# Attention values in transposed float32r form, with the order of all instructions from the kernel's own list schedule

## The chip, the cores and the metric

The kernel runs on one core of a Trainium2 chip. The metric is the device time of one execution in microseconds. Three runs of the kernel before took 700.12, 702.43 and 703.76 us; their median is 702.43 us.

## The reference

One layer of a hybrid decoder, float32, 512 tokens of 1024 features. Cut to what matters here:

```python
h = modulate(rms_norm(x, pre_norm_mix), sh1, sc1)          # shift and scale from silu(c) @ ada_w + ada_b
z = h @ w_in                                               # gate, x, q, 3 x (k, v), attention gates
rnn = gelu(g_rnn) * rg_lru(conv4(x_rnn))
# attention: 8 query heads, 2 key/value heads of 64 features; three branches, each with its own softmax
o = g0 * softmax(q kc^T - alibi) @ vc                      # 31 compressed blocks of keys
  + g1 * softmax(q ks^T - alibi) @ vs                      # selected blocks: all 8 of the 8, causal
  + g2 * softmax(q kw^T - alibi) @ vw                      # window of 512: all, causal
y = concat([rms_norm(rnn, norm_rnn_out), rms_norm(att, norm_att_out)]) @ w_out
x = x + (1 + g1) * rms_norm(y, post_norm_mix)
h = modulate(rms_norm(x, pre_norm_mlp), sh2, sc2)
x = x + (1 + g2) * rms_norm(square(relu(h @ w_ff1)) @ w_ff2, post_norm_mlp)
```

With 512 tokens the top 16 blocks of 64 are all 8 blocks, so the selected branch is plain causal attention.

## The kernel before

All large products are made in parts: a float32 operand is split into a high and a low part in float32r (`split_f32`, line 399), and `mm3` (line 762) sums high x high, high x low and low x high in PSUM. The eight PSUM banks have four names: `f` (2), `s` (3), `pv` (1), `tp` (2).

The work has five stages: a first wave (`first_wave`, line 689: norm of x, modulation, and the first columns of the input projection, bound to the arrival of the modulation's weights); then projections, recurrent branch, attention and output projection; then the MLP's first product (`up_first`, `up`), its second (`down_all`), and the last norm (`finish`).

Attention is cut into 16 units, in the order of `UNITS`: a key head g, a tile i of 128 tokens, and a pair of query heads. `att_scores` (line 1194) makes for each head of the pair the scores of the three branches side by side (compressed, selected, window), with the mask and the slope added and the row maxima taken by VectorE (`mx`), then `Exp` on ScalarE with the row sums in `sm`. `den` is the gate over the row sum. The probabilities `p` lie with tokens on partitions and are not normalised. `att_values` (line 1249) transposes blocks of 128x128 of `p` on TensorE into a bank `tp`, up to four blocks a bank, and `evac` (line 472) copies them to `pt` in float32 on ScalarE or VectorE, whichever is sooner free. The product takes `pt` as the stationary operand and moves a block of values, 64 columns, float32; it leaves tokens on partitions, and the three branches and two heads side by side in one bank `pv`. VectorE multiplies the bank by `den` into `tmp`, and GpSimd adds the three branches into `att`. At most two units are scored ahead of the values. `att_finish` (line 1297) takes the sum of squares of a tile of `att` by `Square` with accumulation, transposes the tile, and ScalarE and VectorE write the high and low parts with the norm's gain (`Q[k]`, `Q[4 + k]`, whose buffers are free by then). `projections` (line 924) multiplies these by `w_out`; the residual and the second norm follow, and `turn_h` (line 1331) transposes the result and writes the MLP's input in parts `h2` and `h2l`.

The order: class `Clocks` (line 51) keeps an estimated time for each engine. Every instruction goes through `issue` (line 167), by `mm` (216), `turn` (222), `act` (225), `elem` (236) or `load` (266), each with a cost formula. `pace` (line 203) doubles TensorE's cost in a window that follows an idle one. Streams (generators) of instructions are chosen by `run_streams` (line 291) for the one TensorE can start first; `Weights` (line 316) runs loads and splits ahead of use. After the first wave instructions are recorded, and `flush` (line 118) emits them by a key: 0.7 of the estimated start less 0.3 of the length of the longest chain that follows. There are three flushes: after the attention, after the first MLP columns, and at the end. Up to the end of the first wave the kernel holds the tile framework's manual schedule open (`start_ctx`), so that this part stays in the order of emission; after it the framework's scheduler orders what it is given. Each engine then runs its own queue in that order.

Of the kernel before, what the change touches and what calls it, by code (L numbers as in the profile page):

```python
# [38 lines left out]
# the order of the input projection's columns and of the compression's weights, and that of the attention's units  # L39
# [4 lines left out]
# sets of activation tables that have a function  # L44
# [3 lines left out]
WINDOW = 4096 / 1200.0  # L48


class Clocks:
    """What each engine has been given so far, in estimated microseconds: every instruction goes through here
    on its way to the engine, and the order of emission is chosen by these clocks."""

    def __init__(self, nc):
        self.nc = nc
        self.free = dict.fromkeys(("pe", "act", "dve", "pool", "dma", "dge"), 0.0)
        self.boxes = {}
        self.base = {}
        self.slots = {}  # L60
        self.table = None
        self.windows = {}
        self.nodes = None
        self.name = ""
        self.uses = {}
        self.before = {}

    # -- tiles --
    def tile(self, pool, tag, bufs, shape, dtype, name):
# [3 lines left out]
        if len(ring) < bufs:  # L73
            self.base[key] = 0.0
        else:
            old = ring.pop(0)
            self.base[key] = self.last(old)
            self.boxes.pop(old, None)
            self.before[key] = old
# [25 lines left out]
    def ready(self, *aps):  # L105
        """when what these hold has been written"""
# [11 lines left out]
    def flush(self):  # L118
        """emit what was recorded, what has most left to come first"""
        nodes, self.nodes = self.nodes, []  # L120
        tail = [0.0] * len(nodes)
        for k in range(len(nodes) - 1, -1, -1):
            eng, cost, prev = nodes[k][:3]
            tail[k] += cost
            for j in prev:
                lag = (SYNC if nodes[j][0] != eng else 0.0) + (DMA_LAT if nodes[j][0] == "dma" else 0.0)
                tail[j] = max(tail[j], tail[k] + lag)
        left = [0] * len(nodes)
        after = [[] for _ in nodes]
        for k, (_, _, prev, _, _, _) in enumerate(nodes):  # L130
            left[k] = len(prev)
            for j in prev:
                after[j].append(k)
        key = [(1 - TAIL) * start - TAIL * tail[k]
               for k, (_, _, _, _, start, _) in enumerate(nodes)]
        heap = [(key[k], k) for k in range(len(nodes)) if not left[k]]
        heapq.heapify(heap)
        while heap:
            _, k = heapq.heappop(heap)
            nodes[k][3]()  # L140
            for j in after[k]:
                left[j] -= 1
                if not left[j]:
                    heapq.heappush(heap, (key[j], j))
        self.uses, self.before = {}, {}

    def put(self, eng, cost, outs, ins, fn):
# [3 lines left out]
        for ap, wr in [(a, False) for a in ins] + [(a, True) for a in outs]:  # L151
            key = ap.tensor.name
            if key not in self.uses:
                self.uses[key] = []
                for u in self.uses.get(self.before.get(key), ()):
                    prev.add(u[5])
# [8 lines left out]
        self.nodes.append((eng, cost, prev, fn, self.start, self.name))  # L165

    def issue(self, eng, cost, outs, ins, fn):
        start = self.free[eng]
        for ap, wr in [(a, False) for a in ins] + [(a, True) for a in outs]:
# [13 lines left out]
        if eng == "pe":  # L183
            cost = self.pace(start, cost)
        end = start + cost
        self.start = start
# [16 lines left out]
    def pace(self, start, cost):  # L203
        """the tensor engine's clock is halved in a window that follows an idle one"""
        k = int(start / WINDOW)
        if self.windows.get(k - 1, 0.0) < 0.5 * WINDOW:
            cost *= 2
        end = start + cost
        while start < end:
            stop = min(end, (k + 1) * WINDOW)  # L210
            self.windows[k] = self.windows.get(k, 0.0) + stop - start
            start, k = stop, k + 1
        return cost

    # -- instructions --
    def mm(self, out, lhs, rhs, start, stop):
        n = out.free_size()
        fast = 1 if rhs.dtype == F32R and n >= 256 else 4
        self.issue("pe", max(n * fast / 2400 + 0.002, 0.1 if fast == 4 else 0.05), [out], [lhs, rhs],
                   lambda: self.nc.tensor.matmul(out, lhs, rhs, start=start, stop=stop))  # L220

    def turn(self, out, src, ident):
        self.issue("pe", out.free_size() / 1175, [out], [src], lambda: self.nc.tensor.transpose(out, src, ident))  # L223

    def act(self, out, src, func, scale=1.0, bias=0.0, accum_out=None):
        ins = [src] + [a for a in (scale, bias) if not isinstance(a, float)]
        outs = [out] + ([accum_out] if accum_out is not None else [])
        cost = 0.05 + out.free_size() / 1200 + 0.043 * (src.space != PSUM) + 0.05 * (len(ins) + len(outs) - 2)
        if func in TABLES and self.table not in TABLES[func]:
# [4 lines left out]
                   lambda: self.nc.scalar.activation(out, src, func, scale=scale, bias=bias, **kw))  # L234

    def elem(self, eng, what, out, *args, **kw):
# [11 lines left out]
        else:  # L248
            cost = 0.165 + n / (480 if len(wide) > 1 else 1000)
# [16 lines left out]
    def load(self, out, src):  # L266
        self.free["dge"] = max(self.free["dge"], 0.0) + 0.47
        self.free["dma"] = max(self.free["dma"], self.free["dge"])
        self.issue("dma", out.free_size() * out.shape[0] * 4 / 360000.0, [out], [src],
# [3 lines left out]
class Stream:  # L273
    """A generator of instructions. Before each step it yields a function for when that step can start."""
# [41 lines left out]
class Weights:  # L316
    """The weights in the order of their use: loads ahead of splits into high and low parts, both ahead of use."""

    def __init__(self, clk, pool):
        self.clk, self.pool, self.jobs, self.index = clk, pool, [], {}  # L320
# [4 lines left out]
    def add(self, name, n, loads, split=True):  # L325
        self.index[name] = len(self.jobs)
        self.jobs.append((name, n, loads, split))
# [21 lines left out]
    def load(self):  # L349
# [4 lines left out]
        self.loaded[name] = raw  # L354
        self.raw_live.append(name)
        self.l += 1

    def split(self):
# [3 lines left out]
        if split:  # L362
            hi = c.tile(self.pool, "hi", PART_BUFS, [P, 1024], F32R, f"hi_{name}")[:, :n]
            lo = c.tile(self.pool, "lo", PART_BUFS, [P, 1024], F32R, f"lo_{name}")[:, :n]
            split_f32(c, hi, lo, raw[:, :n])
            self.parts[name] = (hi, lo)
            self.raw_live.remove(name)
            self.part_live.append(name)
# [13 lines left out]
    def when(self, name, k=None):  # L382
        """when the weights of a job can be used"""
# [10 lines left out]
    def drop(self, name):  # L394
        """nothing more reads this job's tiles"""
        (self.part_live if self.jobs[self.index[name]][3] else self.raw_live).remove(name)


def split_f32(c, hi, lo, src):
    """src = hi + lo exactly, both with the short mantissa of float32r"""  # L400
# [12 lines left out]
def block_kernel(tc, x, c, ada_w, ada_b, pre_norm_mix, w_in, conv_w, conv_b, lru_wa, lru_ba, lru_wx,  # L413
# [52 lines left out]
    def p_tile():  # L466
        return small(mp, "p", 4, [P, K_END])

    def pt_tile(dt):
        return small(mp, "pt", 4, [P, 512], dt)  # L470
# [13 lines left out]
    def after(ev, fn=None):  # L484
        """a step's start: once an event has happened, and then what fn says"""
# [28 lines left out]
    # k - q, with the mask of the future; the same for the compressed keys  # L514
# [10 lines left out]
    # tokens that see a whole compressed block  # L525
# [23 lines left out]
    def rstd_of(ss, width):  # L549
        """(ss / width + eps) ** -0.5"""  # L550
# [8 lines left out]
    V = [mp.tile([P, 4, 64], F32, name=f"V{t}") for t in range(NT)]  # L559
    VC = [mp.tile([32, 64], F32, name=f"VC{g}") for g in range(2)]  # L560
# [32 lines left out]
    for hf_ in range(2):  # L593
        for n in range(2):
            for k2 in range(2):
                r0 = hf_ * 512 + k2 * 256
                W.add(f"o{hf_}{n}{k2}", 1024, [(lambda r: r.rearrange("p (k c) -> p k c", k=2),
                                               w_out[r0:r0 + 256, half(n)].rearrange("(k p) c -> p k c", p=P))])
# [6 lines left out]
    def norm_x(t, h=None):  # L605
        """the squares' sum of a tile of tokens (half h of it), then the tile normed, features 0 first"""
# [19 lines left out]
    def warm(n):  # L626
        """keep the tensor engine's clock up while the first norm waits for its data"""
# [26 lines left out]
    def ada_sums(j):  # L654
        """shift and scale of features j, from the sums of the rows of each partition"""
# [16 lines left out]
    def prep_h(j, at, pt, sa, rest=None):  # L672
        """the tokens' features j, modulated; the sums for the next ones in between"""
# [85 lines left out]
    start_ctx.close()  # L759
# [35 lines left out]
    # rows (parity of the token, feature), columns (k or v, group, token)  # L795
# [54 lines left out]
    def values():  # L850
        for t in range(NT):
# [13 lines left out]
            act(V[t], src, AF.Copy)  # L865
# [5 lines left out]
    def compress(v, l4):  # L871
        """hidden units of the compressed keys and values, transposed"""
# [15 lines left out]
    def compress_out():  # L888
# [12 lines left out]
        for g in range(2):  # L901
            act(VC[g], pc2[:32, 64 * g:64 * g + 64], AF.Copy)
# [21 lines left out]
    def projections():  # L924
        for hf_ in range(2):
# [561 lines left out]
```

## Time and profile before

| | |
|---|---|
| runs | 700.12, 702.43, 703.76 us |
| span of the profiled execution (the only time that it has) | 700.8 us |
| instructions in the profile | 9072 |
| DMA | 85.10 MB, 121 GB/s mean |
| attention's value products | 384 instructions of 64 columns, two for each of 192 products |
| transposes of probabilities | 192 |

Engines are PE (TensorE), PEld (its weight loads), DVE (VectorE), ACT (ScalarE), POOL (GpSimd) and SP (SyncE, which issues the transfers). A row of a group is: line, engine, operation, names out<-in, shapes, count | busy us, mean ns | idle time of the engine just before, with what ended it. The names are those of the tiles, without numbers. Most instructions have the line of a helper (L220 matmul, L223 transpose, L234 ScalarE, L255 VectorE and GpSimd), so the tile names tell them apart. A row of a window is: from:to and its length, busy us and count for PE, PEld, DVE, ACT and POOL, the granted clock of TensorE (1.00 is full speed), the DMA share, GB/s. A row of the timeline is: start, duration, engine, line, operation, names, count, and in brackets the idle time before it. A row of the chain is: start, us, engine, tile and line, count. Banks `f`, `s`, `pv` and `tp` appear in products of several stages.

### The profile page before, as it was taken

Reading aid. Unit: us, or ns where it says so; the run is one execution under the profiler, and the core shown is the slowest. Engines: PE = TensorE matmul, PEld = TensorE weight load, DVE = VectorE, ACT = ScalarE, POOL = GpSimd, SP = SyncE. Lnnn points to the kernel's source line nnn. Section 1 sums busy time; section 2 is a strip of 40 time slices with the busy share of each in tenths; the row PEclk is TensorE's granted clock in tenths of the full one; section 3 lists DMA queues with packets and bytes.
Section 4 is the critical chain, followed back from the end, with each engine's and each line's share of the span. In section 5 each row is a group of like instructions: output and inputs, shape, how many; then the busy total and the mean of one; then the engine's idle time right before and its main releaser. Section 6 shows DMA issues by size and latency. Waiting matters only on the chain.

```text
span 700.8 us, 9072 instructions
## 1 busy us (share of the span) xinstructions
PE 654.4 (93%) x3350; PEld 543.0 (77%) x3350; DVE 414.2 (59%) x788; ACT 267.6 (38%) x553; POOL 157.9 (23%) x148
## 2 busy tenths in 40 slices
PE   3888899894999999998899999999999999999995
PEld 3666788474888889897898888888888888888884
DVE  5998974678688856684895374343353333333334
ACT  4335424584686665565441111111122332222221
POOL 4232010337225201222234343333410000000001
PEclk9999999897999999999999999999999999999999
DMA  8985668642435510001556353432323222223102
GB/s 272 271 249 158 181 206 235 206 130 85 132 111 157 201 35 27 1 0 55 157 151 180 90 151 93 118 91 91 102 97 101 91 91 90 91 91 96 55 18 102
DMA packets 89971, 85.10 MB, mean 121 GB/s; under 512 B 5172, under 2 KB 71876, under 8 KB 89928
## 3 DMA queue, kind: packets, MB, share of 16 engines
q1 hardware_dynamic: 89928, 84.54, 39.6%
q8 instruction: 26, 0.43, 0.3%
q14 instruction: 17, 0.14, 0.1%
HBM read 82.43 MB, written 2.10 MB: 121 GB/s over the span
## 4 chain that ended last, share of the span: by engine, by line
PE 49%; DVE 1%; ACT 0%; issue 0%; POOL 0%; DVEq 0%; POOLq 0%
PE f L220 28%; PE s L220 11%; PE tp L220 7%; PE pv L220 4%; DVE r L255 1%; PE tp L223 0%; ACT ar L234 0%; POOL stat L255 0%; ACT r L234 0%; DVEq L1483 0%; POOLq L1483 0%; DVE h2l L255 0%; DVE stat L255 0%
## 5 line engine op out<-in xcount | busy, mean ns | idle before, releaser
L220 PE MATMUL f<-h,hi_f 128*128 128x512 f32 x224 | 83.4, 393 | 0.0
L220 PE MATMUL f<-h,lo_f 128*128 128x512 f32 x224 | 82.7, 389 | 0.0
L220 PE MATMUL f<-h2l,hi_f 128*128 128x512 f32 x224 | 82.6, 389 | 0.0
L255 POOL TENSOR_TENSOR fT<-fT 128x512 f32<-128x512 f32 x32 | 57.9, 1812 | 107.3 <-ACT fT L234 107.3
L255 DVE TENSOR_TENSOR fl<-fT,fh 128x512 fp32r<-128x512 f32 x28 | 19.3, 690 | 88.1 <-ACT fh L234 88.1
L234 ACT ACTIVATE fT<-f 128x512 f32<-128x512 f32 x28 | 16.8, 600 | 126.1 <-PE f L220 126.1
L234 ACT ACTIVATE fh<-fT 128x512 fp32r<-128x512 f32 x28 | 17.7, 632 | 105.1 <-PE f L220 103.3
L255 POOL TENSOR_SCALAR stat<-stat 128x1 f32<-128x1 f32 (+1 forms) x21 | 7.8, 373 | 218.7 <-DVE stat L255 182.3
L255 DVE CAST hi_f<-raw_f 128x1024 fp32r<-128x1024 f32 x24 | 18.0, 749 | 63.5 <-PE f L220 63.5
L234 ACT ACTIVATE p<-p,mx 128x32 f32<-128x32 f32 (+4 forms) x96 | 45.3, 473 | 26.1 <-DVE mx L255 25.9
L255 DVE SCALAR_TENSOR_TENSOR accT<-ar,sil,accT 128x512 f32<-128x512 f32 x56 | 50.0, 892 | 6.5 <-DMA ar<-in_ada_w 5.9
L255 DVE TENSOR_TENSOR lo_d<-raw_d,hi_d 128x1024 fp32r<-128x1024 f32 x32 | 40.2, 1255 | 15.7 <-ACT hi_d L234 15.3
L220 PEld LDWEIGHTS f<-h,hi_f 128*128 128x128 f32 x224 | 42.1, 188 | 9.1 <-issue 0.5
L220 PEld LDWEIGHTS f<-h2l,hi_f 128*128 128x128 f32 x224 | 42.0, 188 | 9.1 <-issue 0.5
L220 PEld LDWEIGHTS f<-h,lo_f 128*128 128x128 f32 x224 | 42.1, 188 | 8.8
L220 PEld LDWEIGHTS pv<-V,pt 128*128 128x128 f32 x320 | 44.8, 191 | 2.9 <-ACT pt L234 0.5
L220 PE MATMUL pv<-V,pt 128*128 128x64 f32 x320 | 44.4, 260 | 0.2 <-ACT pt L234 0.2
L220 PE MATMUL s<-K,Q 128*128 128x288 f32 (+4 forms) x128 | 35.3, 346 | 9.5 <-DVE mx L255 9.5
L255 DVE TENSOR_TENSOR lo_f<-raw_f,hi_f 128x1024 fp32r<-128x1024 f32 x30 | 40.7, 1357 | 3.9 <-ACT hi_f L234 1.3
L223 PE MATMUL tp<-ident,p 128*128 128x128 f32 (+1 forms) x192 | 40.6, 279 | 0.7 <-DVE h L255 0.7
L220 PE MATMUL s<-hi_d,fh 128*128 128x512 f32 x84 | 33.3, 396 | 0.0
L220 PE MATMUL s<-hi_d,fl 128*128 128x512 f32 x84 | 33.3, 396 | 0.0
(259 smaller groups left out, 1607.4 us busy)
## 6 DMA issues: line engine op xcount, KB each, us to landing
ar<-in_ada_w SPq DMA_DIRECT2D x32, 512.0 KB, 5.4
raw_f<-in_w_ff SPq DMA_DIRECT2D x32, 512.0 KB, 4.1
raw_d<-in_w_ff SPq DMA_DIRECT2D x32, 512.0 KB, 3.2
p<-in_ada_w SPq DMA_DIRECT2D x32, 256.0 KB, 3.8
raw_o<-in_w_out SPq DMA_DIRECT2D x8, 512.0 KB, 4.3
r<-in_x SPq DMA_DIRECT2D x7, 512.0 KB
raw_a<-in_w_in SPq DMA_DIRECT2D x8, 320.0 KB, 5.2
raw_x<-in_w_in SPq DMA_DIRECT2D x4, 512.0 KB
```

The source lines that it names most:

```text
L220: lambda: self.nc.tensor.matmul(out, lhs, rhs, start=start, stop=stop))
L223: self.issue("pe", out.free_size() / 1175, [out], [src], lambda: self.nc.tensor.transpose(out, src, ident))
L234: lambda: self.nc.scalar.activation(out, src, func, scale=scale, bias=bias, **kw))
L255: self.issue(eng, cost, outs, ins, lambda: fn(out, *args, **kw))
```

## The change

1. **Scaling first.** After `den`, each of the three branches of both heads' `p` is multiplied by its column of `den` (`scaled`), on GpSimd, VectorE or ScalarE, by the clocks. That is 96 instructions: 49 on VectorE, 29 on ScalarE, 18 on GpSimd.
2. **Values transposed.** V and the compressed values VC are kept as high and low parts side by side, 128 columns in float32r. Per block the two heads' probabilities are transposed beside each other (at most two blocks, 512 columns, in a bank); ScalarE writes the high part, VectorE the bank less the high part. The product takes the values (64 columns high, 64 low) as the stationary operand and moves the high, then the low part of the probabilities, 256 columns for two heads; all three branches add up in one accumulation. Partitions 0 to 63 hold what the high part of the values gave, partitions 64 to 127 what the low part gave: ScalarE copies the latter out (`oc`), and VectorE adds both into `att`, which now has features on partitions.
3. **The end of the attention.** `att` needs no transpose any more. ScalarE squares it, GpSimd adds, and a product with a column of ones gives the sum of squares. The gain of the norm goes into the split of the weights of the output projection (`gains` in `Weights`).
4. **Buffers.** Six tiles of `p` and `pt` instead of four, four of `mx`, `sm` and `den` instead of three; up to three units ahead.
5. **Order.** `flush` is a list schedule: it runs all engines by estimated time, each takes from what is ready the instruction with the longest chain after it, and ScalarE avoids a change of its function table. `pace` is gone, the cost formulas have other constants. The manual schedule stays open to the end, so the order of emission is the order of the queues. The first wave keeps its order. After it TensorE goes through pairs of projection columns in alternation; in the MLP's first product the two banks `f` advance in alternation and end close together (before, most of one came first); in the second each column's 24 products go through all eight banks three times, high x high, then low x high, then high x low; at the end the two halves of the last tokens finish together.

```diff
     def flush(self):
...
+        for _ in range(n - first):
+            best = None
+            for e, t in self.real.items():
+                if soon[e]:
+                    at = t
+                elif wait[e]:
+                    at = max(t, wait[e][0][0])
+                else:
+                    continue
+                if best is None or at < best[0]:
+                    best = at, e
+            at, e = best
+            while wait[e] and wait[e][0][0] <= at + 0.01:
+                _, k = heapq.heappop(wait[e])
+                heapq.heappush(soon[e], (-tail[k], k))
+            if e == "act":
+                k = self.pick_act(soon[e], nodes)
+            else:
+                _, k = heapq.heappop(soon[e])
...
+            self.real[e] = self.fin[k] = at + cost
             nodes[k][3]()
...
+    def scaled(seg, col):
+
+        n, f = seg.free_size(), clk.free
+        r = clk.ready(seg, col)
+        cost = {"pool": 0.165 + n / 1000, "dve": 0.125 + n / 1900, "act": 0.14 + n / 1200}
+        eng = min(cost, key=lambda e: max(f[e], r) + cost[e])
+        if eng == "act":
+            act(seg, seg, AF.Copy, scale=col)
+        else:
+            clk.elem(eng, "tensor_scalar", seg, seg, col, None, op0=ALU.mult)
...
     def att_values():
...
-                    for k, (e, _, c0, _, _, _) in enumerate(sub):
-                        turn(tp[:w, tok(k)], scored[u][0][e][:, c0:c0 + w], ident)
-                    pt = pt_tile(F32)[:w, :P * len(sub)]
-                    evac(pt, tp[:w, :P * len(sub)])
-                    turned.append((pt, sub))
+                    for k, (c0, _) in enumerate(sub):
+                        for e in range(2):
+                            turn(tp[:, tok(2 * k + e)], scored[u][e][:, c0:c0 + P], ident)
+                    w = 256 * len(sub)
+                    hi, lo = pt_tile(F32R)[:, :w], pt_tile(F32R)[:, :w]
+                    act(hi, tp[:, :w], AF.Copy)
+                    dve("tensor_sub", lo, tp[:, :w], hi.bitcast(F32))
+                    turned.append((hi, lo, sub))
...
-                    for k, (e, si, _, v, first, last) in enumerate(sub):
-                        mm(po[:, si, e, :], pt[:, tok(k)], v, first, last)
-            den = scored[u][1]
-            tmp = small(mp, "tmp", 2, [P, 3, 2, 64])
-            dve("tensor_mul", tmp, po, den.unsqueeze(3).to_broadcast([P, 3, 2, 64]))
-            o = att[i][:, (4 * g + 2 * pair) * 64:(4 * g + 2 * pair) * 64 + P].rearrange("p (e d) -> p e d", e=2)
-            pool("tensor_add", o, tmp[:, 0], tmp[:, 1])
-            pool("tensor_add", o, o, tmp[:, 2])
+                    for k, (_, v) in enumerate(sub):
+                        sl = slice(k * 256, k * 256 + 256)
+                        mm(po, v, hi[:, sl], done == 0, False)
+                        done += 1
+                        mm(po, v, lo[:, sl], False, done == n)
+            o = att[i][:, tok(2 * g + pair)]
+            oc = small(mp, "oc", 2, [64, 256])
+            act(oc, po[64:128, :], AF.Copy)
+            for e in range(2):
+                dve("tensor_add", o[64 * e:64 * e + 64], po[0:64, tok(e)], oc[:, tok(e)])
...
     def att_finish():
...
+            sq = cmt[:, 0:512]
+            act(sq, att[t], AF.Square)
+            hi, lo = h_tile(), h_tile()
+            act(hi, att[t], AF.Copy)
+            dve("tensor_sub", lo, att[t], hi.bitcast(F32))
+            for w in (256, 128):
+                pool("tensor_add", sq[:, 0:w], sq[:, 0:w], sq[:, w:2 * w])
...
+            mm(ps[:, 0:1], sq[:, 0:P], ones[:, 0:1], True, True)
```

More of the change, by code (lines that the diff above doesn't have):

```diff
@@ L75, in tile @@
         else:
-            old = ring.pop(0)
+            old = ring.pop(next(k for k, v in enumerate(ring) if v not in self.live))
             self.base[key] = self.last(old)
@@ L118, in flush @@
     def flush(self):
-        nodes, self.nodes = self.nodes, []
-        tail = [0.0] * len(nodes)
-        for k in range(len(nodes) - 1, -1, -1):
+        first, nodes = self.emitted, self.nodes
+        self.emitted = n = len(nodes)
+        tail, left = {}, {}
+        after = {k: [] for k in range(first, n)}
+        for k in range(n - 1, first - 1, -1):
             eng, cost, prev = nodes[k][:3]
-            tail[k] += cost
+            tail[k] = tail.get(k, 0.0) + cost
+            left[k] = 0
@@ L136, in flush @@
[L136 to L139, printed above, removed]
+                if j >= first:
+                    left[k] += 1
+                    after[j].append(k)
+                    tail[j] = max(tail.get(j, 0.0), tail[k] + self.lag(nodes[j][0], eng))
+        ready = {k: max([0.0] + [self.fin[j] + self.lag(nodes[j][0], nodes[k][0]) for j in nodes[k][2] if j < first])
+                 for k in range(first, n)}
@@ new lines, in flush @@
+        soon = {e: [] for e in self.real}
+        wait = {e: [] for e in self.real}
+        for k in range(first, n):
+            if not left[k]:
+                heapq.heappush(wait[nodes[k][0]], (ready[k], k))
+        for _ in range(n - first):
[17 more added lines that the diff above has]
+                _, k = heapq.heappop(soon[e])
+            cost, func = nodes[k][1], nodes[k][4]
+            if func in TABLES and self.real_table not in TABLES[func]:
+                self.real_table = TABLES[func][0]
+                cost += 1.3
+            self.real[e] = self.fin[k] = at + cost
@@ L152, in put @@
             key = ap.tensor.name
[L153 to L156, printed above, removed]
+            self.uses.setdefault(key, [])
+            if wr:
+                prev.update(u[5] for u in self.uses.get(self.before.get(key), ()))
             p0, p1, lo, hi = self.box(ap)
@@ L354, in load @@
         self.loaded[name] = raw
+        self.clk.live.add(raw.tensor.name)
         self.raw_live.append(name)
@@ L924, in projections @@
     def projections():
+        for g in range(2):
+            clk.zero(VC[g].bitcast(F32))
         for hf_ in range(2):
```

163 lines of the change are left out of this document (86 added, 77 removed).

## The prediction

> **What bounds the kernel now.** I read the page's head first, then the busy times by stage, then the shares of the chain that ended last.
>
> ```profile
> span 700.8 us, 9072 instructions
> PE 654.4 (93%) x3350; PEld 543.0 (77%) x3350; DVE 414.2 (59%) x788; ACT 267.6 (38%) x553; POOL 157.9 (23%) x148
> PE 49%; DVE 1%; ACT 0%; issue 0%; POOL 0%; DVEq 0%; POOLq 0%
> 0.00:68.00 68.00, 50.47 (x234) 40.23 (x234) 57.13 (x121) 27.23 (x42) 20.87 (x27) 0.97 0.83 245
> 68.00:361.00 293.00, 271.11 (x1675) 231.79 (x1674) 216.98 (x518) 169.35 (x406) 76.57 (x82) 0.96 0.40 119
> 361.00:515.00 154.00, 154.00 (x677) 126.79 (x676) 72.79 (x75) 20.98 (x35) 56.49 (x31) 1.00 0.40 118
> 515.00:693.00 178.00, 178.00 (x768) 143.85 (x767) 64.41 (x73) 48.67 (x68) 3.27 (x7) 1.00 0.25 82
> ```
>
> The stage rows give, after the length: PE, weight loads, DVE, ACT, POOL busy, then the granted clock, the DMA share and GB/s. TensorE bounds the kernel: PE is busy 93% of the span, and the two MLP stages (361 to 693) have no idle PE at all at clock 1.00. Only in 68 to 361, which holds the input projections, the attention and the output projection, is there something to win: 293 us, of which 22 without PE, at a mean clock of 0.96. The first 68 us are the same instructions in both kernels. So the question is when the last part of the MLP's input, the last `h2l`, is written; from there TensorE runs dense. The profiled span of 700.8 lies 1.6 below the median of the three runs, 702.4; I add my differences to the median.
>
> **The change on TensorE.** It replaces the value products. Before, 192 f32 products of 64 columns are 384 instructions; after, 96 blocks go through two float32r products (high, low part) of 256 columns, 192 instructions.
>
> ```profile
> L220 PE MATMUL pv<-V,pt 128*128 128x64 f32 x320 | 44.4, 260 | 0.2 <-ACT pt L234 0.2
> L220 PE MATMUL pv<-VC,pt 32*128 32x64 f32 x64 | 11.9, 287 | 0.0
> 79.83 3.68 PE L220 MATMUL s<-r,raw_c 128*128 128x64 f32 x32
> 355.18 5.88 PE s L220 x49
> L220 PE MATMUL s<-K,Q 128*128 128x288 f32 x48 | 12.7, 327 | 9.5 <-DVE mx L255 9.5
> ```
>
> Means overlap on PE, so I take start to start: 32 f32 instructions of 64 columns in 3.68 us, 0.115 each (0.11 without the last one's tail); 49 float32r instructions of 256 columns in 5.88, 0.12 each. 384 x 0.11 = 42.2 us become 192 x 0.12 = 23.0: 19 us less. The transposes of probabilities stay 192; the 16 of the attention output go (about 1.7 us), and four f32 products with a column of ones come (about 0.9). TensorE's work falls by some 20 us. Further, the 9.5 us wait of the first scores' products for DVE's `mx` may shrink: DVE then stood in the recurrent branch; counted along the two orders with the rows' durations, 49 us of its work stand between the first wave and the first maximum where 69 stood. That would be worth 30 us, if the vector engines kept up. So the sum is made on DVE.
>
> **The change on DVE.**
>
> ```profile
> 64.00:354.00 290.00, 268.11 (x1634) 227.81 (x1633) 213.67 (x525) 167.53 (x404) 73.84 (x80) 0.96 0.40 119
> 353.46 0.75 DVE L255 TENSOR_TENSOR h2l<-h,h 128x256 fp32r<-128x256 f32 x2
> L255 DVE COPY pt<-tp 128x512 f32<-128x512 f32 x13 | 8.9, 684 | 4.5 <-PE tp L223 4.4
> L255 DVE COPY pt<-tp 32x256 f32<-32x256 f32 x4 | 1.6, 410 | 1.2 <-PE tp L223 1.2
> L255 DVE TENSOR_TENSOR tmp<-pv,den 128x384 f32<-128x384 f32 x16 | 8.9, 556 | 10.8 <-PE pv L220 9.2 <-issue 1.6
> L255 DVE SCALAR_TENSOR_TENSOR Q<-tp,col,Q 128x128 fp32r<-128x128 f32 x16 | 4.5, 344 | 4.8 <-ACT Q L234 4.8
> L255 DVE TENSOR_TENSOR h<-pt,h 128x512 fp32r<-128x512 f32 x8 | 5.5, 686 | 0.0
> L255 DVE CUSTOM_DVE_ANT_0 p<-s,tab 128x256 f32<-128x256 f32 x16 | 6.7, 416 | 0.7 <-PE s L220 0.6
> L255 DVE TENSOR_SCALAR p<-p 128x512 f32<-128x512 f32 x4 | 1.6, 420 | 0.0
> L255 DVE TENSOR_SCALAR r<-r,stat 128x128 f32<-128x128 f32 x1 | 0.3, 288 | 0.7 <-POOL stat L255 0.7
> L255 DVE TENSOR_TENSOR K<-tp,K 128x32 fp32r<-128x32 f32 x2 | 0.3, 187 | 0.0
> L255 DVE SCALAR_TENSOR_TENSOR r<-f,stat,r 128x512 f32<-128x512 f32 x8 | 6.0, 748 | 1.0 <-PE f L220 1.0
> L255 DVE TENSOR_TENSOR lo_o<-raw_o,hi_o 128x1024 fp32r<-128x1024 f32 x8 | 9.8, 1220 | 1.6 <-ACT hi_o L234 1.6
> 348.73 0.75 DVE L255 TENSOR_TENSOR h2l<-h,h 128x256 fp32r<-128x256 f32 x2
> 349.40 0.99 DVE L255 TENSOR_SCALAR h<-tp,a,s 128x256 f32<-128x256 f32 x2
> ```
>
> Removed: 8.9 + 1.6 + 8.9 + 4.5 = 23.9 us, all in four groups. Added: 40 low parts of transposed probabilities of 512 columns at 0.69 and 16 of 256 at 0.42, 34.1; 49 of the 96 scalings of probabilities (16 of 32 columns at 0.19, 9 of 128 at 0.29, 8 each of 256 and 384 at 0.35 and 0.42, 8 of 512 at 0.48), 15.8: this operation with a column of `den` is not in the trace, the 512-wide one lies between the 0.420 of `p<-p` (two constants) and 0.69 (two tensors), and I take the low end because a single tensor is read; at the high end it would be 5 us more. 32 additions of 64x128 at 0.29 (as 128 columns), 9.3. Small ones, 10.3: eight `lo_o` halves at 0.75 for four whole ones at 1.22 (+1.1), four low parts of the attention output (2.8), four of V (1.7), the compressed values, four sums' copies and weight splits that ACT and POOL did before (4.7). Together 69.5 - 23.9 = 45.6. But DVE instructions overlap a little: the pair at 348.73 ends at 349.48 and the next starts at 349.40. With 0.07 for each of some 111 more instructions, 37.8 remain.
>
> So DVE has 213.7 + 37.8 = 251.5 us of work from 64 us to the last `h2l`, which ends now at 354.2 (290 us, 74% busy). TensorE's part of the same stretch becomes 268 - 20 = 248 us busy. Both engines now carry about the same; DVE, whose queue is in order and which also waits for ACT's high part before each low part, sets the end. What share can it reach? The trace shows both ends:
>
> ```profile
> 70.00:90.00 20.00, 17.81 (x95) 15.37 (x95) 19.16 (x33) 9.28 (x15) 2.84 (x1) 0.91 0.58 168
> 200.00:220.00 20.00, 20.00 (x128) 17.32 (x128) 16.34 (x63) 14.37 (x51) 9.66 (x11) 1.00 0.37 107
> 168.00:322.00 154.00, 151.12 (x992) 132.51 (x993) 110.20 (x358) 97.93 (x293) 37.55 (x57) 0.98 0.27 84
> ```
>
> Where it has a queue of ready work it is 96% busy (19.16 of 20); in the densest stretch of the attention, where TensorE sets the pace, 82% (16.34 of 20). At 96% the last `h2l` comes at 64 + 251.5 / 0.96 = 326, 28 us earlier; at 82% at 371, 16.5 later; 87% is the point of no change. I take 90%, between the two, since more units are in flight (three instead of two, six buffers of probabilities instead of four) and the queue is thus fuller: 64 + 279.4 = 343.4, 10.8 earlier.
>
> ACT gets 13 more evacuations of 512 columns, 16 of 256, 16 of 64x256 and 32 scalings, by my estimate 38 us in the attention, whose row shows 98 of 154 us: about 136 us in a stretch that begins earlier (the first maximum comes after 49 us of DVE work, not 69). It stays below DVE, and costs nothing unless its order is bad. POOL loses 32 additions and gets 18 scalings and 8 small sums: lighter. SyncE issues as many transfers as before, in another order (the modulation's rows earlier, a quarter of the queries' weights ahead of the gate's last ones); the DMA share of 0.40 in the stage row hides that, and if a weight came late, TensorE would pass no other work and lose the delay in full.
>
> For a rule that speaks against this division of the scalings:
>
> ```profile
> 167.06 2.28 DVE L255 TENSOR_TENSOR lo_q<-raw_q,hi_q 128x1024 fp32r<-128x1024 f32 x1
> ```
>
> This one took 2.28 us where `lo_o`, the same shape, takes 1.22. The Trainium skill, "SBUF — State Buffer", section "SBUF: two separate sides", says that a VectorE instruction with two SBUF inputs, or in a mode with two ports, and a GpSimd instruction exclude one another for their whole length. The trace agrees in kind. By that rule the 18 scalings on POOL would stand in DVE's way; at an estimated 0.4 us each the sum would be 7 us worse.
>
> **Attention's end and the MLP.** After the last value product of the attention the four transposes and eight parts with the gain go, and the gain moves into the weights' split, earlier. A few us of latency go with them, but DVE's 25 us of work behind it stay, so I count nothing. In the MLP the same instructions come in another order: two banks of the first product advance in lockstep and end three or four products apart.
>
> ```profile
> 422.58 0.62 PE L220 MATMUL f<-h,lo_f 128*128 128x512 f32 x2
> 423.24 0.60 ACT L234 ACTIVATE fT<-f 128x512 f32<-128x512 f32 x1 [6.20 <-PE f L220]
> 426.79 88.45 PE f L220 x390
> ```
>
> A product takes 88.45 / 390 = 0.227. From the start of the last (422.81, the second of the pair) to the end of ACT's copy (423.84) pass 1.03 us; the new order leaves five products, 1.13 us, before the bank is needed. It just fits: no cost. At the end two halves of the last tokens finish together rather than one after the other, so one more ACT square of about 0.6 us stands behind the last product: +0.6. The sum is -10.8 + 0.6 = -10.2: 702.4 - 10.2 = **692.2 us**.
>
> **Rivals.** (1) *Everything is fed*: DVE reaches 96%, the 9.5 us wait goes, TensorE keeps its 20 us: 702.4 - 28 + 0.6 = 675. For it: DVE does 96% where it is fed. Against: DVE never was over 82% within the attention. Chance 0.14. (2) *DVE's in-order queue becomes the bound below 87%* (slower): a low part waits at the head of the queue for ACT's high part, behind it stand the maxima of the next unit, for which ACT waits. At 82% the time is 702.4 + 16.5 + 0.6 = 719.5, and it decides from 87% on. The clock speaks for it:
>
> ```profile
> 322.30:325.70 3.40, 1.86 (x9) 1.10 (x9) 0.52 (x2) 2.31 (x8) 1.65 (x4) 1.00 0.30 108
> 325.70:329.10 3.40, 3.40 (x9) 2.63 (x10) 2.57 (x8) 1.41 (x2) 0.00 (x0) 0.50 0.00 0
> ```
>
> A stretch with PE busy 1.86 of 3.4 us is followed by one at clock 0.50. A TensorE that waits a little everywhere may be halved often; 0.96 over 293 us is already 12 us of lost clock. The Trainium skill, "TensorE: Matmul & The Clock Gate", section "Part 1: The HAM clock gate", lets the clock fall after an idle window of about 3.4 us; the trace agrees on the length, but here a half-filled window was enough. By the page, short waits would cost no clock. Chance 0.26. (3) *Lockstep stalls the MLP*: if ACT is held by another part of 0.6 us when a bank ends, each of 28 columns loses about 0.5 us, 14 in all: 706; it decides once ACT is over 0.1 us late. Chance 0.14. That the products don't get cheaper is excluded by the 0.12 us row.
>
> **How the numbers follow.** The forecast, DVE at 87 to 94%, has 0.46. A measurement of this kernel tells about 0.5% (3.5 us) from no change. Faster: 0.41 of the forecast's 0.46 and all 0.14 of (1), 0.55. Within: 0.05 of the forecast, 0.05 of (2), 0.02 of (3), 0.12. Slower: 0.21 of (2), 0.12 of (3), 0.33. The range goes from 96% to 82%: 675 to 719.
>
> **What would show it.** DVE's share between 64 us and the last `h2l`, near 90%, and that `h2l` near 343; PE losing its idle time to DVE and ACT low parts (`pt`) rather than to `mx`; value products at 0.12 start to start; no idle PE and clock 1.00 in the MLP, 332 us long. The sum is wrong if DVE's new instructions sit beside waits of TensorE that stay (last `h2l` before 330), or if the MLP is longer than 335 us.

## The result

The changed kernel is slower: 725.67 us (722.51 to 728.51, four runs) against 702.55 us (four runs, one more than in the table above), a ratio of 1.034 [1.029, 1.038]. The forecast was 692.2, with a range from 675 to 719. The profiled execution is one of 722.91 us, with a span of 721.1. The four runs lie at 722.5 to 722.9 and at 728.4 to 728.5; in several kernels with the list schedule the profile shows the first wave ending some 3.5 us later, so part of such a spread comes from there, and the traces below are compared from its end.

The page of the changed kernel, and its windows by the stages of the prediction:

```profile
span 721.1 us, 8884 instructions
PE 649.1 (90%) x3150; PEld 532.1 (74%) x3150; DVE 463.0 (64%) x898; ACT 290.2 (40%) x601; POOL 150.3 (21%) x142
PE 67%; DVE 18%; DMA 4%; ACT 4%; issue 4%; POOL 2%; SPq 1%; DVEq 0%; POOLq 0%; ACTq 0%
0.00:68.00 68.00, 50.67 (x234) 40.41 (x234) 54.22 (x108) 26.37 (x41) 19.76 (x28) 0.97 0.85 246
68.00:361.00 293.00, 247.22 (x1335) 206.05 (x1335) 243.28 (x620) 184.07 (x445) 74.58 (x72) 0.91 0.36 109
```

TensorE was busy for 271 of the 293 us before and for 247 now, at clock 0.91 instead of 0.96, and the stage isn't over at 361. Its dense MLP (the products on all 512 tokens, in which TensorE hardly idles) begins at 378.4, 17.3 us later than before (361.1). Up to the end of the first wave nothing differs (68.0 and 67.6 for the start of its last product), and the MLP costs 3 us. So 17 of the 20 us between the two profiles lie between 68 and 378. The windows of the stretch to the last `h2l` (ends at 370.8):

```profile
64.00:168.00 104.00, 88.55 (x445) 72.95 (x443) 77.10 (x148) 56.83 (x104) 15.24 (x10) 0.92 0.61 182
168.00:320.00 152.00, 135.68 (x769) 112.57 (x770) 139.70 (x429) 109.79 (x310) 45.61 (x45) 0.94 0.26 77
320.00:371.00 51.00, 37.00 (x226) 33.61 (x225) 32.80 (x59) 20.91 (x38) 13.73 (x18) 0.80 0.15 42
64.00:371.00 307.00, 261.22 (x1437) 219.13 (x1436) 249.61 (x634) 187.53 (x451) 74.58 (x72) 0.91 0.36 107
```

VectorE's work is what was forecast, 249.6 us (251.5). Its share is not: 81% over the whole, made of 74% before the attention is in swing, 92% in it (139.7 of 152), and 64% after it. The clock fell to 0.80 in that last part. I read the granted clock of five kernels in windows of 0.2 us, from the first wave's end to the dense MLP; half clock is a granted clock of 0.50. (The last three are experiments, below.)

| kernel | last value product | first `h2l` | dense MLP | us at half clock |
|---|---|---|---|---|
| before | 321.5 | 327.1 | 361.1 | 24.2 |
| changed | 325.5 | 350.0 | 378.4 | 54.6 |
| new arithmetic, old order | 330.3 | 339.5 | 371.4 | 47.6 |
| old arithmetic, new order | 334.1 | 340.8 | 378.4 | 47.6 |
| the same, first recorded first | 321.3 | 327.4 | 364.6 | 23.8 |

The changed kernel's own account from 68 on: TensorE is idle for 46 us instead of 22 (+24). It is busy for 40.8 us at half clock instead of 19.3; if a product takes twice as long there, this costs 11 more. Its work, with the half-clocked time counted half, is 244 us instead of 262 (-18, where 20 were forecast). That makes 17, and 17.3 were seen.

### The profile page after: what moved, and what is told of

Its sections match the earlier page's. It is cut to its first block, busy times and chain, and to the rows that moved or that the text cites. A ratio compares the mean times of both kernels' runs of the same rounds, so it can differ in the third digit from the quotient of the medians.

```text
span 721.1 us, 8884 instructions
## 1 busy us (share of the span) xinstructions
PE 649.1 (90%) x3150; PEld 532.1 (74%) x3150; DVE 463.0 (64%) x898; ACT 290.2 (40%) x601; POOL 150.3 (21%) x142
## 4 chain that ended last, share of the span: by engine, by line
PE 67%; DVE 18%; DMA 4%; ACT 4%; issue 4%; POOL 2%; SPq 1%; DVEq 0%; POOLq 0%; ACTq 0%
PE f L252 38%; PE s L252 15%; PE tp L252 7%; PE pv L252 5%; DVE accT L287 4%; DVE r L287 4%; DVE p L287 4%; DVE pt L287 2%; DMA p<-in_ada_w 2%; PE tp L255 2%; ACT p L266 1%; POOL p L287 1%; DMA r<-in_x 1%; DVE h L287 1%; POOL stat L287 1%
## 5 line engine op out<-in xcount | busy, mean ns | idle before, releaser
L252 PE MATMUL f<-h,hi_f 128*128 128x512 f32 x224 | 73.0, 396 | 0.6 <-ACT hi_f L266 0.6
L252 PE MATMUL f<-h,lo_f 128*128 128x512 f32 x224 | 72.1, 392 | 0.0
L252 PE MATMUL f<-h2l,hi_f 128*128 128x512 f32 x224 | 71.5, 390 | 0.0
L287 DVE CAST hi_f<-raw_f 128x1024 fp32r<-128x1024 f32 x24 | 25.9, 1077 | 53.7 <-PE f L252 53.7
L266 ACT ACTIVATE p<-p,mx 128x512 f32<-128x512 f32 (+4 forms) x96 | 45.3, 474 | 12.8 <-DVE mx L287 12.3
L255 PE MATMUL tp<-ident,p 128*128 128x128 f32 x192 | 39.2, 290 | 10.2 <-DVE pt L287 5.0
L266 ACT ACTIVATE hi_d<-raw_d 128x1024 fp32r<-128x1024 f32 x28 | 29.8, 1066 | 41.1 <-PE f L252 41.1
L252 PE MATMUL f<-hi_o,h 128*128 128x512 f32 x128 | 44.4, 434 | 0.8 <-ACT r L266 0.8
L255 PEld LDWEIGHTS tp<-ident,p 128*128 128x128 f32 x192 | 24.1, 145 | 18.7 <-DVE pt L287 6.3
L266 ACT ACTIVATE pt<-tp 128x512 fp32r<-128x512 f32 (+1 forms) x56 | 29.5, 534 | 19.1 <-PE tp L255 17.7
```

What stands on the lines that cost most here:

```text
L255: self.issue("pe", 0.109, [out], [src], lambda: self.nc.tensor.transpose(out, src, ident))
L287: self.issue(eng, cost, outs, ins, lambda: fn(out, *args, **kw))
```

## The experiments

Theory A: VectorE's added work costs the time whatever the order. Theory B: the list schedule's order costs it. The first two kernels take the change apart.

**Arithmetic alone.** The clock class of before (key, `pace` and cost formulas) put back into the changed kernel; of its edit only a few lines are shown:

```diff
+        key = [(1 - TAIL) * start - TAIL * tail[k]
+               for k, (_, _, _, _, start, _) in enumerate(nodes)]
...
+        if eng == "pe":
+            cost = self.pace(start, cost)
...
     first_wave()
+    start_ctx.close()
     clk.record()
...
     clk.flush()
-    start_ctx.close()
     ctx.close()
```

> Only the new arithmetic (scaling first, values transposed in parts, no transposes of the attention output, larger buffers) under the old order: the old clock class with its key, pace and costs, manual schedule closed after the first wave. Theory A (the added VectorE work, 38 us, costs the time whatever the order): slower than before, 715 to 730. Theory B (the list schedule's order costs it, at the two ends of the attention): about as before or faster, 690 to 705. If both hold, some 708 to 715.

Measured: 713.12 us, ratio 1.017 [1.014, 1.019], 10.9 us slower than before, in the range for both theories at once. Its windows before the attention is in swing, in it, and over the whole stretch to its last `h2l`:

```profile
64.00:168.00 104.00, 87.71 (x447) 69.86 (x445) 77.48 (x129) 52.68 (x80) 26.05 (x13) 0.94 0.60 180
168.00:320.00 152.00, 137.20 (x750) 114.90 (x751) 141.00 (x449) 115.11 (x340) 44.13 (x48) 0.92 0.27 84
64.00:364.50 300.50, 262.13 (x1438) 218.28 (x1437) 246.90 (x631) 188.28 (x455) 79.58 (x72) 0.92 0.38 115
```

VectorE is 93% busy in the attention (141.0 of 152) and 82% over the whole (246.9 of 300.5), under the old order too.

**Order alone.** The changed kernel's clock class in the kernel before, the manual schedule open to the end.

> Only the new order (list schedule, new costs, manual schedule to the end), with the arithmetic and the buffers of before. Theory A (VectorE's added work): about as before, 698 to 705. Theory B (the order): slower, 715 to 725. If the order by itself helps and VectorE's work then hides it: below 698.

Measured: 723.76 us, ratio 1.032 [1.029, 1.036], 21.5 slower, with no new arithmetic at all. Both theories hold, and they don't add: together they cost 23. Its windows from the end of its first wave to the dense MLP show that VectorE's load isn't the reason here (117 of 164 us in the attention); TensorE idles 25 us in all, some 4 more than before. Most of the rest is clock: 47.6 us at half for 24.2 before, of which TensorE was busy for 42.2 and 19.3, so by halving some 11 us more. A further 3 us lie in the first wave and 3 in the MLP. The windows:

```profile
71.00:170.00 99.00, 86.87 (x428) 71.36 (x428) 72.45 (x130) 56.51 (x91) 15.09 (x9) 0.89 0.55 161
170.00:334.20 164.20, 158.58 (x992) 135.66 (x992) 117.19 (x354) 91.79 (x274) 42.49 (x58) 0.94 0.26 81
334.20:378.40 44.20, 36.59 (x256) 34.20 (x255) 25.74 (x48) 18.54 (x34) 10.83 (x12) 0.92 0.17 48
```

**No scaling on GpSimd.**

```diff
-        cost = {"pool": 0.165 + n / 1000, "dve": 0.125 + n / 1900, "act": 0.14 + n / 1200}
+        cost = {"dve": 0.125 + n / 1900, "act": 0.14 + n / 1200}
```

> The changed kernel with no scaling on GpSimd: 96 scalings on VectorE and ScalarE alone. In the changed kernel the 18 scalings on GpSimd took 1.19 us on average, three times my estimate, and stand 8 us long on the chain that ended last. Theory A (VectorE's sum of work is the bound): slower by 2 to 5 us than the changed kernel, since VectorE takes some of them. Theory C (GpSimd's scalings are late and hold VectorE's port): faster by 4 to 8 us.

Measured: 726.97 us (1.036 [1.030, 1.041]), within the runs' spread (721.68 to 730.57) no different from the changed kernel. From the end of the first wave to the dense MLP both traces take the same (310.7 and 310.8 us). The slow scalings on GpSimd were on the chain, yet cost nothing that shows; theory C's 4 to 8 us faster did not appear, nor did theory A's 2 to 5 slower beyond that spread.

**The low part left out, under both orders.** The probabilities are used in their high part alone:

```diff
-                    dve("tensor_sub", lo, tp[:, :w], hi.bitcast(F32))
...
-                        mm(po, v, hi[:, sl], done == 0, False)
                         done += 1
-                        mm(po, v, lo[:, sl], False, done == n)
+                        mm(po, v, hi[:, sl], done == 1, done == n)
```

> The changed kernel without the low part of the transposed probabilities: 56 subtractions on VectorE (34 us) and 96 products of 256 columns (11.5 us of TensorE) left out; the rest stays. Theory A (VectorE's work bounds the attention): 25 to 34 us faster than the changed kernel. If TensorE or the chain of one unit bounds it: 5 to 12 us faster. If the ends alone cost the time (theory B, the attention itself hidden): under 5 us.

> The new arithmetic under the old order, without the low part of the transposed probabilities (56 VectorE subtractions, 34 us, and 96 products, 11.5 us, left out). If VectorE's sum bounds the attention under the old order: 20 us or more under the 713 of the arithmetic alone, so 685 to 693. If the chain of one unit and the clock bound it, as under the list schedule, where the same cut gave 7 us: 704 to 709.

Measured: 718.84 us under the new order (1.024 [1.020, 1.027]), 6.8 less than the changed kernel; 693.69 us under the old one (0.989 [0.986, 0.992]), 19.4 less than the arithmetic alone and so just short of the 20 expected. The same cut of 34 us of VectorE and 11.5 of TensorE is worth three times as much under the old order. So there VectorE's sum probably lies on the path, and under the list schedule something else does; how much of the 19.4 is TensorE's part isn't separated here. The second of these is faster than both kernels, 8.8 us under before; its price is that the low part's contribution is missing from the value sums. Its windows from 64 us to its last `h2l`:

```profile
64.00:168.00 104.00, 86.34 (x443) 67.94 (x441) 78.51 (x125) 52.07 (x78) 27.88 (x14) 0.94 0.59 177
168.00:306.00 138.00, 122.26 (x693) 101.14 (x693) 114.06 (x403) 119.28 (x349) 45.84 (x49) 0.96 0.29 92
306.00:344.00 38.00, 30.27 (x196) 27.36 (x197) 24.19 (x48) 16.60 (x29) 9.69 (x11) 0.91 0.33 97
```

With VectorE relieved (114 of 138) ScalarE is the busiest of the vector engines (119 of 138), and TensorE still idles for 16 of 138.

**No scalings, old order.** The call of `scaled` left out, so the values aren't normalised.

> The new arithmetic under the old order, without the 96 scalings of the probabilities (left out; 49 of them by the rows about 16 us of VectorE, the others on ScalarE and GpSimd). If VectorE's sum is on the path there, as the cut of the low part showed (34 us of it gave 19.4): about 8 to 11 us under 713, so 702 to 705. If the scalings hide: 710 to 713.

Measured: 703.27 us (1.001 [0.999, 1.003]), 9.8 less than the arithmetic alone. Without the 96 scalings the loss of the new arithmetic under the old order is gone. They are no work of TensorE, so under this order the load of the engines that feed it does lie on the path.

**The clock in the tail.** Theory D: idle time costs twice, since the clock halves after it. The longest wait behind the attention in the timeline of the changed kernel, and below it the windows from there on:

```profile
325.49 0.39 PE L252 MATMUL pv<-pt,VC 128*128 128x256 f32 x1 [0.74 <-DVE pt L287]
332.27 0.58 PE L252 MATMUL tp<-ones,cmt 128*128 128x1 f32 x2 [6.39 <-POOL cmt L287]
```

```profile
328.60:332.00 3.40, 0.00 (x0) 0.00 (x0) 2.68 (x4) 1.72 (x4) 2.47 (x4) 0.50 0.00 0
332.00:335.40 3.40, 3.13 (x8) 2.57 (x9) 0.92 (x2) 0.00 (x0) 0.96 (x3) 0.50 0.02 5
335.40:338.80 3.40, 3.40 (x9) 2.64 (x8) 0.00 (x0) 1.01 (x2) 0.00 (x0) 0.50 0.00 0
```

```diff
+FILL = 40
...
+            ocr = small(mp, "oc", 2, [64, 256], F32R)
...
+            act(ocr, po[64:128, :], AF.Copy)
+            late["oc"] = ocr
...
+            if t == NT - 1:
+                for _ in range(FILL):
+                    mm(ps[:, 256:512], late["oc"][:, 0:P], late["oc"], True, True)
             mm(ps[:, 0:1], sq[:, 0:P], ones[:, 0:1], True, True)
```

> The changed kernel with 40 float32r products of 256 columns (4.8 us at full clock), of no use, in TensorE's queue behind the last value product, where it now stands idle for 6.4 us, and ahead of the product with the ones. Theory D (the half clock after idle windows is a part of the loss): the half-clocked 10 us from 328.6 shrink, 3 to 6 us faster than the changed kernel. If the clock doesn't matter there: no change, or up to 1 us slower.

The timeline and the windows of the same stretch with the filler:

```profile
324.92 5.05 PE L253 MATMUL tp<-oc 64*128 64x256 f32 x40 [0.47 <-ACT oc L267]
331.20 0.38 PE L253 MATMUL tp<-ones,cmt 128*128 128x1 f32 x2 [1.23 <-POOL cmt L288]
```

```profile
328.20:331.60 3.40, 2.17 (x18) 1.96 (x18) 3.29 (x4) 0.68 (x1) 2.87 (x3) 0.99 0.00 0
331.60:335.00 3.40, 3.40 (x9) 2.63 (x10) 0.93 (x3) 0.47 (x2) 1.49 (x4) 0.51 0.00 0
335.00:338.40 3.40, 3.40 (x16) 2.76 (x15) 0.00 (x0) 2.01 (x2) 1.42 (x1) 1.00 0.00 0
```

The half clock shrinks from 10.2 to 3.4 us, and the products from the one with the ones to the first transposes of the residual take 7.5 us (331.20 to 338.67) instead of 8.9 (332.27 to 341.17). That is 1.4 us, not the 3 to 6 expected; the median, 725.03 (720.09 to 729.06), can't show it. The clock is part of the loss, but this wait alone is worth little.

**TensorE's work given back.** Each transpose of probabilities made twice.

> The changed kernel with each of the 192 transposes of probabilities made twice into the same place: 21 us of TensorE work given back, nothing else. If TensorE's saved 20 us were lost as idle time and half clock (theory D): under 8 us slower, perhaps none. If TensorE's work still sets the pace in the attention: 15 to 21 us slower.

Measured: 733.01 us (1.043 [1.040, 1.046]), 7.3 slower than the changed kernel for 21 us of work. Two thirds of what TensorE is spared there are lost again: with the work given back its idle time up to the dense MLP falls from 46 to 38 us, and its busy time at half clock from 41 to 33.

**Who makes the order.** The manual schedule closed after the first wave, the list schedule kept:

> The changed kernel with the manual schedule closed after the first wave, as before the change, so that the framework orders what the list schedule emits. If the queues' order made by the list schedule itself is what loses 12 to 21 us: within 5 us of the changed kernel only if the framework keeps it; since the two orders differ in thousands of places, I expect 708 to 716, near the arithmetic under the old order (713). If the emission order decides all the same: 723 to 728.

Measured: 727.61 us (1.037 [1.034, 1.040]): no gain, although in the trace 1124 of TensorE's 3150 instructions are, by their tile names, others than in the changed kernel at the same place. So the manual schedule is not what costs. Then one line of the list schedule, in both kernels that have it:

```diff
-                heapq.heappush(soon[e], (-tail[k], k))
+                heapq.heappush(soon[e], (k, k))
```

> The new order alone (arithmetic of before), with one edit: among the ready instructions each engine takes the one recorded first, not the one with the longest chain behind it. Theory E (longest chain first puts the residual of the first tokens behind the attention of the last ones, so that the MLP's first products, 23 us, can start only at the end, and it mixes f32 products and waits): the first h2l comes near the last value product again and the time falls from 723.8 to 700 to 712. If what costs is the loss of the clock model or the manual schedule: 720 to 728.

> The same edit on the changed kernel. By theory E it falls from 725.7 to near the arithmetic under the old order, 705 to 716; else it stays at 720 to 730.

Measured: 707.52 us (1.008 [1.005, 1.011]) instead of 723.76, and 715.26 us (1.017 [1.012, 1.023]) instead of 725.67. So 16 of the order's 21 us, and by the medians 10 of the changed kernel's 23, come from the rule "longest chain first". (The two profiled executions of the changed kernel without and with this edit lie only 5.4 us apart.)

Theory E's forecast came, but not by the late residual. In the order alone the first `h2l` comes 6.7 us after the last value product with the rule and 6.1 without it (5.6 before), and from the last value product to the dense MLP it is 44.3 and 43.3 us. Of the 14 us by which the dense MLP comes earlier, 13 lie ahead of the last value product (334.1 against 321.3), 3 of these in the first wave. What went with the rule is half clock, 47.6 to 23.8 us, of which TensorE was busy for 42.2 and 17.9, so some 12 us; its idle time stayed (25 and 26 us). The 3 us in the MLP went too. One place where the two differ is TensorE's first work behind the first wave, with the rule and without it:

```profile
74.25 8.34 PE L252 MATMUL s<-r,raw_c 128*128 128x64 f32 x38 [3.79 <-DVE r L287]
70.36 0.70 PE L252 MATMUL f<-h,hi_x 128*128 128x512 f32 x2 [1.89 <-DVE Q L287]
```

With the rule the clock is halved there for 13.6 us, without it not at all before 109.6 us. That fits the theory's other half, f32 products mixed with waits, at this one place. In the changed kernel the residual of the first tokens is indeed late, the first `h2l` 24.5 us after the last value product. With the edit it is 7.4 us, but the last value product moves from 325.5 to 334.1, and the dense MLP only from 378.4 to 375.7. The half clock is 47.8 us there, as with the arithmetic under the old order.

**The clock model off** in the kernel before (TensorE's planned cost never doubled).

> The kernel before with one edit: the planner's clock model is off (TensorE's planned cost is never doubled after an idle window); key, costs and schedule as before. The change drops this model, and the kernels with the list schedule spend 45 to 60 us at half clock instead of 24. If the missing model is what loses the clock: 708 to 715. Theory E (the longest chain first is what loses it, the model matters little): 700 to 706.

Measured: 702.74 us (1.001 [0.999, 1.003]). The dropped model isn't the cause.

## Why the prediction was wrong

**TensorE: right.** The value products fell to 192 with 0.12 to 0.13 us each, its work fell by 18 us by the account above, and giving 21 us back costs only 7. It was also right that DVE's first maxima come earlier (133.9 instead of 169 us) and that this wait then bounds less, but the wait came back behind it, as the timeline of TensorE shows:

```profile
169.26 1.01 PE L252 MATMUL s<-K,Q 128*128 128x256 f32 x3 [8.54 <-DVE mx L287]
```

**VectorE's sum: right** (249.6 against 251.5 us), made of groups near their estimates:

```profile
L287 DVE TENSOR_TENSOR pt<-tp,pt 128x512 fp32r<-128x512 f32 x40 | 27.0, 684 | 3.3 <-ACT pt L266 2.4 <-issue 0.8
L287 DVE TENSOR_TENSOR att<-pv,oc 64x128 f32<-64x128 f32 x32 | 8.9, 279 | 0.3
L287 DVE TENSOR_SCALAR p<-p,den 128x512 f32<-128x512 f32 x8 | 4.4, 548 | 0.1
L287 POOL TENSOR_SCALAR p<-p,den 128x512 f32<-128x512 f32 x4 | 7.3, 1820 | 22.6 <-ACT pt L266 13.3 <-DVE den L287 9.2
```

The scalings took 19.6 us on VectorE for my 15.8. On GpSimd they took 0.88 to 1.82 us, where I had put 0.4. The page of the Trainium skill that was weighed there, "SBUF — State Buffer", section "SBUF: two separate sides", with its exclusion between VectorE and GpSimd, would make some of them slow, and they are; how much of it is that exclusion is not shown, since they are slower the wider they are, too. Taking them off GpSimd changed nothing, so its 7 us do not appear.

**The share of 90%: the step that failed.** It was laid over the whole stretch from 64 us to the last `h2l`, as if work could be moved freely in it. In the attention VectorE did reach 92%. Before it, VectorE waits (74% busy), as it did before the change (80 of 104 us): in the trace 12.8 us for ScalarE's high part of weights, which in turn waits for their load, and much of the rest for loads and projections. After it, a chain of short steps runs for each tile of tokens (64%). The new order isn't needed for this: with the arithmetic alone the share is 82%, below the 87% of no change, and the time 10.9 us up instead of 10.2 down. These 21 us are the larger part of the 33 by which the forecast missed.

**The order: counted at 0.6 us, worth 21 by itself.** I took the list schedule as neutral beyond VectorE: ScalarE was to cost "nothing unless its order is bad", and for the end of the attention I wrote "so I count nothing". It puts first what has the longest chain behind it, and that one rule is 16 of the 21 us. In the old arithmetic it costs clock rather than idle time: without it the half clock falls from 47.6 us to 23.8, and TensorE's idle time stays. On top of the new arithmetic the order adds 12.6 us (713.12 to 725.67). There the first tokens' half of the MLP's first products (23 us in all) is at hand from 350 us instead of 327, but the experiments don't show what this costs: with the rule removed it comes at 341.5, and the dense MLP 2.7 us earlier.

**The rivals.** The first, everything fed, did not come. The second, VectorE's queue, had the right sign and nearly the right numbers, a share of 82% and a last `h2l` at 371 (81% and 370.8). This is luck in part: its queue was to hold VectorE up in the attention, where the share was 92%; the idle time lies before and after it. What it said of the clock happened: 54.6 us at half clock. The Trainium skill, "TensorE: Matmul & The Clock Gate", section "Part 1: The HAM clock gate", calls for a whole idle window; the trace of the filler shows a window of 2.17 busy us of 3.4 followed by one at 0.51, so here again it needs less. The third, lockstep in the MLP, fell: no stall between the banks. The MLP's 3 us are a wait of 1.5 for `g2row` at 538 and slots of 0.229 instead of 0.227 us (133.46 us for 583 products on the chain), 1.4 over some 670 products. The MLP's 335.5 us (332.3 before) just passed the prediction's second sign of a wrong sum; with the rule "longest chain first" removed, the 3 us are gone.

**Open.** What the remaining 5 us of the order without that rule are was not tried, nor what the late residual costs by itself, nor a division of the low parts with GpSimd. Why the two costs, 10.9 and 21.5 us, make only 23 together is not shown. A version with all of the arithmetic that beats the kernel before wasn't found.

## What to carry to other kernels

A new order of instructions is not neutral because the work is the same: run it alone, on the old arithmetic. Here it cost 21 us, some 11 of them by the clock and only 4 by idle time. A share of busy time belongs to a stage; before it is laid over a stretch, ask in each part of it what the engine waits for. And a saving on the engine that bounds is worth only what the engines that feed it can follow: here one group of subtractions, 34 us of VectorE, with its products of 11.5, decided between 693.7 and 713.1 under the old order.

## What was not expected of the hardware

The half clock does not end with full windows alone. In the changed kernel it lasts three windows from 72.6 us, two of them filled with float32 products of 64 columns, and ends after one with float32r products of 512; before, with the float32r products first, it lasted one. Whether the type or the number of columns counts isn't separated. The timeline and the windows of the changed kernel:

```profile
71.81 8.06 PE L252 MATMUL s<-r,raw_c 128*128 128x64 f32 x40 [3.76 <-DVE r L287]
79.64 1.20 PE L252 MATMUL f<-h,hi_x 128*128 128x512 f32 x2
```

```profile
69.20:72.60 3.40, 0.79 (x7) 0.82 (x8) 3.31 (x7) 3.31 (x5) 0.00 (x0) 1.00 0.05 20
72.60:76.00 3.40, 3.40 (x18) 3.40 (x18) 3.35 (x5) 3.31 (x6) 2.36 (x1) 0.50 0.03 5
76.00:79.40 3.40, 3.40 (x18) 3.40 (x18) 3.33 (x6) 1.75 (x4) 0.00 (x0) 0.50 1.04 302
79.40:82.80 3.40, 3.40 (x12) 2.82 (x12) 3.35 (x6) 0.74 (x1) 0.00 (x0) 0.50 0.92 314
82.80:86.20 3.40, 3.40 (x26) 3.15 (x25) 3.25 (x8) 1.49 (x2) 0.00 (x0) 1.00 0.63 187
```

At half clock these products take 0.20 us each (40 in 8.06), at full clock 0.115 in the kernel before.
